# Modulation's products on GpSimd, their sums a step later on ScalarE

## The chip, the cores and the metric

One core of a Trainium2 chip runs the kernel. The metric is device time in microseconds. The core's engines each work through an instruction queue of their own: TensorE (PE; its weight loads are listed as PEld), VectorE (DVE), ScalarE (ACT), GpSimd (POOL) and SyncE (SP), which issues nearly all DMAs.

## What is computed

Two blocks follow each other on a sequence of 256 positions of width 1024. The first has two layers: a retention layer (4 heads, chunks of 128) and a causal latent-attention layer (16 heads, low-rank queries and keys); after each comes a normalised residual and a gated per-layer embedding, `x + (p @ w_proj) * sigmoid(x @ w_gate)`. The second block is modulated: six vectors of 1024 come from a conditioning vector c, and scale, shift and gate what follows.

```python
mod = jax.nn.silu(c) @ w_ada[l] + b_ada[l]
sh1, sc1, g1, sh2, sc2, g2 = jnp.split(mod, N_MOD, axis=-1)
h = layer_norm(x) * (1.0 + sc1[:, None]) + sh1[:, None]
proj = h @ w_in[l]
...
x = layer_norm(ALPHA * x + g1[:, None] * mix, ln1_g[l], ln1_b[l])
h = layer_norm(x) * (1.0 + sc2[:, None]) + sh2[:, None]
```

The change concerns the first line alone. `silu(c) @ w_ada` is a product of one row with a matrix of 1024 x 6144. Its first result is needed when the second block starts; the values of the second half of the block are needed late.

## The kernel before

Activations lie transposed: 128 features on the partitions, 256 positions along the free axis, in blocks of two or four such tiles. Every large matrix product in fp32 is made of three matmuls in a rounded format: each operand is split into a rounded part `hi` and the rest `lo`, and `mm` (L235ff) multiplies hi by hi, hi by lo and lo by hi. For each 128x1024 tile of weights SP loads `raw` (L165), ACT rounds it to `wh` (L178), and DVE subtracts to `wl` (L179); each has five or six buffers. Activations are split in the same way (L187 on ACT, L188 on DVE).

Modulation is not done on PE. `ada_steps` is a generator of 48 steps. Each holds one 128x1024 tile of the modulation weights (`adach`, two buffers, loaded over SP in program order), in which each partition has one output's 1024 weights. One DVE instruction multiplies it by silu(c), which lies in `siluc` on all partitions, and sums along the row into one column of `mod` (L413); after each eighth column the bias is added (L418). A call of `ada()` takes the next step; the very first call only issues two loads.

When a step comes is set by a clock that the program keeps while it is written down: `tick` adds each matmul's estimated time, and calls `ada()` when `mods["rate"]` microseconds of it have passed since the last step, up to a limit of 41 calls. `mod_rate` sets the rate at each stage: 10 at the start, 1.8 in the out-projection of the retention layer, 7.61 and then 12.84 in latent attention, 2.27 in its out-projection. A loop ahead of the second block takes what is left up to the limit, and `late_steps` takes eight further calls during the last stage. The final order on each engine is made by a scheduler from this program order and the dependencies; loads marked `keep_in_program_order` keep theirs on SP.

In the profiled execution 26 of the 48 L413 run in the first 204 us (start and retention layer), 16 in the latent-attention layer up to 397 us, none between there and 759 us, and six from there to 813 us.

The names in the rows: `ps` is a PSUM bank, `half` an activation block or half of a split, `t` a temporary, `sm` a softmax tile, `mod` the modulation's columns, `xs` (in the code) the input of the second block scaled by modulation, `php` the split per-layer embedding.

Of the kernel before, what the change touches and what calls it, by code (L numbers as in the profile page):

```python
# [14 lines left out]
AF = mybir.ActivationFunctionType  # L15
ALU = mybir.AluOpType
ADD, SUB, MUL = ALU.add, ALU.subtract, ALU.mult
# [65 lines left out]
def tile_kernel(ctx, tc, order, xT, pT, pos, vec, cst, cv, rows, wada, wts, outT):  # L83
    nc = tc.nc
    V, A, T = nc.vector, nc.scalar, nc.tensor
# [11 lines left out]
    def nm(s):  # L97
        uid[0] += 1
        return f"{s}_{uid[0]}"
# [26 lines left out]
    def two(nb):  # L126
        return Blk(nb, F32R), Blk(nb, F32R)
# [29 lines left out]
    def fetch(entries, width, parts=True, step=D, pinned=False):  # L157
        g = len(order)
        order.append((width, list(entries)))
        n = len(entries) * width  # L160
        tag, bufs = (("raw", 6), ("wh", 5), ("wl", 5))[0 if parts else [0, 1][g % len([0, 1])]]
        raw = wp.tile([P, D], F32, tag=tag, name=nm("raw"), bufs=bufs)
        for o in range(0, n, step):
            e = min(n, o + step)
            d = nc.sync.dma_start(out=raw[:, o:e], in_=wts[g, :, o:e])  # L165
            if pinned:
                tc.keep_in_program_order(d)
        return raw[:, :n]
# [13 lines left out]
    def nouter(name, ms, kbs, c0=0):  # L182
        return [(name, kb * P, c0 + m * P) for m in ms for kb in kbs]
# [15 lines left out]
    clk = [0.0]  # L199
# [3 lines left out]
    def after(us, fn):  # L203
        queue.append((clk[0] + us, fn))
        queue.sort(key=lambda e: e[0])


    mods = {"rate": None, "last": 0.0, "n": 0}

    def mod_rate(us):  # L210
        mods["rate"], mods["last"] = us, clk[0]

    def tick(us):
        clk[0] += us
        if busy[0]:
            return
        busy[0] = True
        if mods["rate"] and clk[0] - mods["last"] >= mods["rate"] and mods["n"] < 41:
            mods["last"] = clk[0]
            ada()  # L220
        while queue and queue[0][0] <= clk[0]:
            queue.pop(0)[1]()
        busy[0] = False

    def drain():
        busy[0] = True
        while queue:
            due, fn = queue.pop(0)
            clk[0] = max(clk[0], due)
            fn()  # L230
        busy[0] = False
# [4 lines left out]
    def mm(ps, l, r, first, last):  # L236
        T.matmul(ps, l[0], r[0], start=first, stop=False)  # L237
        T.matmul(ps, l[0], r[1], start=False, stop=False)  # L238
        T.matmul(ps, l[1], r[0], start=False, stop=last)  # L239
        tick(3 * cols(r[0]) / 2400.0)  # L240
# [5 lines left out]
    def rhs(pair, kb):  # L246
        return pair[0][kb], pair[1][kb]
# [35 lines left out]
    def col(name, i, n=1):  # L283
        o = VOFF[name] + i
        return vc[:, o:o + n]
# [111 lines left out]
        return t.unsqueeze(1).to_broadcast([P, n, S])  # L397


    mod = cp.tile([P, 48], F32, name="mod")  # L400
    sc = cp.tile([P, D], F32, name="siluc")

    def ada_steps():
        def fetch(n):
            ch = sp.tile([P, D], F32, tag="ada1", name=nm("adach"), bufs=2)
            tc.keep_in_program_order(nc.sync.dma_start(out=ch, in_=wada[n * P:(n + 1) * P, :]))
            return ch

        have = [fetch(0), fetch(1)]
        yield  # L410
        for n in range(48):
            ch = have.pop(0)
            V.tensor_tensor_reduce(ch, ch, sc, 1.0, 0.0, MUL, ADD, mod[:, n:n + 1])  # L413
            if n + 2 < 48:
                have.append(fetch(n + 2))
            if n % 8 == 7:
                m = slice(n - 7, n + 1)
                V.tensor_add(mod[:, m], mod[:, m], col("b_ada_2", n - 7, 8))  # L418
            yield

    ada_it = ada_steps()
# [9 lines left out]
    def ada():  # L431
        mods["n"] += 1
        next(ada_it, None)
# [80 lines left out]

    after(12.0, silu_c)
    after(18.0, ada)
    after(30.0, lambda: mod_rate(10))
    after(40.0, trig4)

    ret_g = two(16)  # L520
# [100 lines left out]
    def out_proj(name, pairs, ka, rate, done, layer):  # L621
        ys = proj_banks()
        mod_rate(rate)
        seq = Seq(nouter(name, range(8), range(ka)) + nouter(name, range(8), range(ka, 16)))
        for m in range(8):
            for kb in range(ka):
                mm(ys.at(m), seq.next(), rhs(pairs, kb), ys.starts(m) and kb == 0, False)
        drain()
        mod_rate(None)
        prep = ple_proj(layer)  # L630
        for m in range(8):
            for kb in range(ka, 16):
                mm(ys.at(m), seq.next(), rhs(pairs, kb), False, kb == 15 and ys.ends(m))
            if ys.ends(m):
                done(m, ys)
        return ys, prep
# [83 lines left out]
    def ple_proj(layer):  # L720
        php = [tp.tile([P, 2, S], F32R, tag="fa", name=nm("php"), bufs=3) for _ in range(2)]
        raw = t2()
        nc.gpsimd.dma_start(out=raw, in_=pT[:, 2 * layer:2 * layer + 2, :])
        split(php[0], php[1], raw)

        def prepared():
            seq = Seq(nouter(f"ple_proj{layer}", range(8), range(2)))
            tiles = [seq.next() for _ in range(16)]
            prj = Blk(DB)
            for i in range(4):  # L730
                ps = bank2()
                for b in range(2):
                    for kb in range(2):
                        mm(ps[:, b, :], tiles[(2 * i + b) * 2 + kb], (php[0][:, kb, :], php[1][:, kb, :]), kb == 0, kb == 1)
                A.copy(prj.pair(i), ps)
            return prj
        return prepared

    sums, done = proj_sums(False, lambda m, ys: ys.piece(m), "r")
    ys, prep = out_proj("ret_out", ret_g, 12, 1.8, done, 0)  # L740
    xt = post(xt, ys, sums, 0, prep)


# [78 lines left out]
    def mla_gate(p):  # L822

        if p % 2 == 0:
            sgs[p // 2] = Blk(4)
        ps = bank2()
        for b in range(2):
            for kb in range(8):
                mm(ps[:, b, :], seq_g.next(), rhs(xp, kb), kb == 0, kb == 7)
        gr = t2()  # L830
        V.scalar_tensor_tensor(gr, ps, -0.5, bc2(r1["nr"]), MUL, MUL)
        A.activation(sgs[p // 2].pair(p % 2), gr, AF.Silu)

    mla_g = two(16)
# [104 lines left out]
        V.tensor_mul(gt, pso, sgs[p // 2].pair(p % 2))  # L939
        split(mla_g[0].pair(p), mla_g[1].pair(p), gt)  # L940

    mod_rate(7.61)
    ng = 0
    for p in range(8):
        while ng < [2, 4, 6, 8, 8, 8, 8, 8][p]:
            mla_gate(ng)
            ng += 1
        if p == 4:
            mod_rate(12.84)
        mla_proj(p)  # L950
        after(3.07, lambda p=p: mla_scores(p))

    sums, done = proj_sums(False, lambda m, ys: ys.piece(m), "m")
    ys, prep = out_proj("mla_out", mla_g, 12, 2.27, done, 1)
    xt = post(xt, ys, sums, 1, prep)

    while mods["n"] < 41:
        ada()  # L960
    s1 = cp.tile([P, 16], F32, name="s1")
    ms = cp.tile([P, 16], F32, name="ms")
# [544 lines left out]
```

## Time and profile before

| what | value |
|---|---|
| median of 3 runs | 853.06 us (850.65 to 853.61) |
| the profiled execution, its own time | 847.85 us |
| its span, first to last instruction | 846.1 us |
| mean granted clock of TensorE in it | 0.997 of full speed |
| busy: PE, DVE, ACT, POOL | 826.1, 703.1, 555.2, 9.9 us |
| DMA | 167.48 MB, mean 198 GB/s |

The profile is of one execution. Its tables give an engine's busy time, the idle time ahead of a group of instructions, and what ended that idle time (`<-DVE t L331`: the result t of DVE's instruction of line 331). An engine's idle time matters where PE in turn waits for it.

### The profile page before, as it was taken

The numbers are of one execution on the slowest core, as the hardware profiler recorded it, in microseconds if no ns is written. First come the engines' busy times: TensorE is split into PE (matmuls) and PEld (weight loads), VectorE is DVE, ScalarE is ACT, GpSimd is POOL, SyncE is SP. The second block draws the span as 40 slices with busy tenths as digits, with TensorE's granted clock in tenths as the row PEclk, the third lists the DMA queues.
The fourth block names the chain that finished last, engine by engine and source line by source line (L and its number), as shares of the span: only waits on it lengthen the run. The fifth ranks groups of instructions, "written<-read, shape, count | busy, mean of one in ns | idle before, by whom it ended". The sixth has DMA issues, their size and how long they took to land.

```text
span 846.1 us, 15771 instructions
## 1 busy us (share of the span) xinstructions
PE 826.1 (98%) x6114; PEld 787.9 (93%) x6114; DVE 703.1 (83%) x1283; ACT 555.2 (66%) x968; POOL 9.9 (1%) x30
## 2 busy tenths in 40 slices
PE   8999999999999999998999999999999999999995
PEld 6989999999999989998999999999998999999885
DVE  6999798988889978688874768899677888889986
ACT  7655565545676686777754857999756576666550
POOL 0000000000000000000000000000000000000001
PEclk9999999999999999999999999999999999999998
DMA  9875567778556637374255364245463455567722
GB/s 335 323 258 212 215 217 269 255 264 319 171 182 248 223 145 259 116 263 145 99 184 176 121 224 152 98 150 199 148 224 128 134 190 191 184 214 255 277 77 75
DMA packets 46634, 167.48 MB, mean 198 GB/s; under 512 B 5216, under 2 KB 5472, under 8 KB 46560
## 3 DMA queue, kind: packets, MB, share of 16 engines
q1 hardware_dynamic: 45936, 164.38, 55.1%
q0 software_dynamic: 624, 2.10, 0.9%
q8 instruction: 48, 0.79, 0.4%
q14 instruction: 26, 0.21, 0.1%
HBM read 165.41 MB, written 1.05 MB: 197 GB/s over the span
## 4 chain that ended last, share of the span: by engine, by line
PE 50%; DVE 2%; ACT 1%; issue 1%; DVEq 0%
PE ps L238 13%; PE ps L237 13%; PE ps L239 13%; PE ps L243 10%; PE ps L341 1%; PE ps L363 0%; DVE wl L179 0%; PE ps L920 0%; PE ps L1170 0%; DVE t L1434 0%; DVE sm L1415 0%; DVE half L690 0%; DVE t L1411 0%; DVE t L1412 0%; PE ps L1407 0%
## 5 line engine op out<-in xcount | busy, mean ns | idle before, releaser
L237 PE MATMUL ps<-half,wh 128*128 128x256 f32 x1504 | 425.4, 284 | 1.4 <-ACT half L187 1.4
L238 PE MATMUL ps<-half,wh 128*128 128x256 f32 x1504 | 423.8, 282 | 0.6 <-DVE half L188 0.5
L239 PE MATMUL ps<-half,wl 128*128 128x256 f32 x1504 | 422.0, 281 | 1.1 <-DVE wl L179 1.0
L178 ACT CAST wh<-raw 128x1024 fp32r<-128x1024 f32 x233 | 243.5, 1049 | 154.9 <-PE ps L238 94.8
L179 DVE TENSOR_TENSOR wl<-raw,wh 128x1024 fp32r<-128x1024 f32 x233 | 282.7, 1219 | 59.5 <-ACT wh L178 57.3
L239 PEld LDWEIGHTS ps<-half,wl 128*128 128x128 f32 x1504 | 283.8, 189 | 1.7 <-DVE wl L179 1.7
L238 PEld LDWEIGHTS ps<-half,wh 128*128 128x128 f32 x1504 | 283.4, 188 | 1.9 <-DVE half L188 1.0
L237 PEld LDWEIGHTS ps<-half,wh 128*128 128x128 f32 x1504 | 282.5, 188 | 2.6 <-ACT half L187 2.0
L243 PE MATMUL ps<-half,raw 128*128 128x256 f32 (+2 forms) x384 | 84.9, 380 | 0.0
L243 PEld LDWEIGHTS ps<-half,raw 128*128 128x128 f32 x384 | 72.5, 190 | 10.0
L237 PE MATMUL ps<-wh,half 128*128 128x512 f32 (+1 forms) x202 | 72.6, 360 | 0.9 <-ACT wh L178 0.9
L413 DVE CUSTOM_DVE_ANT_0 adach<-adach,siluc 128x1024 f32<-128x1024 f32 x48 | 58.4, 1218 | 16.7 <-DMA adach<-in_wada 16.7
L238 PE MATMUL ps<-wl,half 128*128 128x512 f32 (+1 forms) x202 | 71.0, 351 | 0.5 <-DVE wl L179 0.5
L239 PE MATMUL ps<-wh,half 128*128 128x512 f32 (+1 forms) x202 | 71.0, 352 | 0.0
L1087 ACT ACTIVATE t<-apad,vec 128x256 f32<-128x256 f32 x106 | 44.3, 501 | 0.5 <-DVE half L1088 0.5
L237 PEld LDWEIGHTS ps<-wh,half 128*128 128x128 f32 x202 | 37.9, 188 | 6.8 <-ACT wh L178 1.7
L238 PEld LDWEIGHTS ps<-wl,half 128*128 128x128 f32 x202 | 38.1, 189 | 6.0 <-DVE wl L179 1.0
L239 PEld LDWEIGHTS ps<-wh,half 128*128 128x128 f32 x202 | 38.0, 188 | 5.6
L1088 DVE TENSOR_TENSOR half<-half,t 128x512 f32<-128x512 f32 x53 | 36.5, 689 | 3.7 <-ACT t L1087 1.8
L187 ACT CAST half<-t 128x256 fp32r<-128x256 f32 (+1 forms) x47 | 20.3, 453 | 17.9 <-DVE t L1347 10.9
L188 DVE TENSOR_TENSOR half<-t,half 128x256 fp32r<-128x256 f32 (+1 forms) x47 | 21.7, 482 | 4.5 <-ACT half L187 3.6
L1342 ACT ACTIVATE t<-ps,vec 128x256 f32<-128x256 f32 x38 | 21.0, 558 | 2.0 <-PE ps L239 1.2
(290 smaller groups left out, 908.1 us busy)
## 6 DMA issues: line engine op xcount, KB each, us to landing
raw<-in_wts SPq DMA_DIRECT2D x257, 512.0 KB, 4.1
adach<-in_wada SPq DMA_DIRECT2D x48, 512.0 KB, 5.0
half<-in_xT SPq DMA_DIRECT2D x4, 256.0 KB, 5.7
half<-in_rows POOLq DMA_DIRECT2D x2, 512.0 KB, 4.7
out<-t SPq DMA_DIRECT2D x4, 256.0 KB, 2.0
cst<-in_cst SPq DMA_DIRECT2D x1, 928.0 KB, 10.6
raw<-in_wts SPq DMA_DIRECT2D x2, 256.0 KB, 4.4
siluc<-in_cv SPq DMA_DIRECT2D x1, 512.0 KB, 9.0
```

The costliest lines, as they stand in the source:

```text
L178: A.copy(hi, raw)
L179: V.tensor_sub(lo, raw, hi.bitcast(F32))
L187: A.copy(hi, src)
L188: V.tensor_sub(lo, src, hi.bitcast(F32))
L237: T.matmul(ps, l[0], r[0], start=first, stop=False)
L238: T.matmul(ps, l[0], r[1], start=False, stop=False)
L239: T.matmul(ps, l[1], r[0], start=False, stop=last)
L243: T.matmul(ps, w, r, start=first, stop=last)
L413: V.tensor_tensor_reduce(ch, ch, sc, 1.0, 0.0, MUL, ADD, mod[:, n:n + 1])
L1087: A.activation(t[:, b, :], apad[:, i0 + b, k:k + S], AF.Copy, scale=w[b])
L1088: V.tensor_add(acc.pair(i0 // 2), acc.pair(i0 // 2), t)
L1342: A.activation(t[:, b, :], ps[:, b, :], AF.Identity, bias=col("b_dw_f_2", m), scale=w[2])
```

## The change

The step is cut in two. GpSimd takes the product, in place: `nc.gpsimd.tensor_mul(ch[n], ch[n], sc)`. At the next step ACT copies the product tile onto itself with an accumulator that sums the row into `mod` (`add_up`), and only then is the load of tile n + 2 issued, into the buffer that has come free. There are therefore 49 steps behind the first call. The limits go from 41 to 42, and the rates change: 10 to 9 at the start, 1.8 to 4.5, 7.61 (and 12.84 from the fifth pair of heads) to 10.5 throughout, 2.27 to 4.5.

```diff
-        if mods["rate"] and clk[0] - mods["last"] >= mods["rate"] and mods["n"] < 41:
+        if mods["rate"] and clk[0] - mods["last"] >= mods["rate"] and mods["n"] < 42:
...
-        have = [fetch(0), fetch(1)]
-        yield
-        for n in range(48):
-            ch = have.pop(0)
-            V.tensor_tensor_reduce(ch, ch, sc, 1.0, 0.0, MUL, ADD, mod[:, n:n + 1])
+        def add_up(n):
+            A.activation(ch[n], ch[n], AF.Copy, accum_out=mod[:, n:n + 1])
             if n + 2 < 48:
-                have.append(fetch(n + 2))
+                ch[n + 2] = fetch(n + 2)
             if n % 8 == 7:
                 m = slice(n - 7, n + 1)
                 V.tensor_add(mod[:, m], mod[:, m], col("b_ada_2", n - 7, 8))
+
+        ch = {n: fetch(n) for n in range(2)}
+        yield
+        for n in range(49):
+            if n > 0:
+                add_up(n - 1)
+            if n < 48:
+                nc.gpsimd.tensor_mul(ch[n], ch[n], sc)
             yield
...
-    after(30.0, lambda: mod_rate(10))
+    after(30.0, lambda: mod_rate(9))
...
-    ys, prep = out_proj("ret_out", ret_g, 12, 1.8, done, 0)
+    ys, prep = out_proj("ret_out", ret_g, 12, 4.5, done, 0)
...
-    mod_rate(7.61)
+    mod_rate(10.5)
...
-        if p == 4:
-            mod_rate(12.84)
...
-    ys, prep = out_proj("mla_out", mla_g, 12, 2.27, done, 1)
+    ys, prep = out_proj("mla_out", mla_g, 12, 4.5, done, 1)
...
-    while mods["n"] < 41:
+    while mods["n"] < 42:
         ada()
```

Lines behind the edit move down by four to six: L789 and L792 become L795 and L798, L697 becomes L703, L735 becomes L741, L1036 becomes L1040. The sum is L411 and the product L424.

Of the 48 steps, 18 now stand in the start and the retention layer, 18 in the latent-attention layer and its out-projection, six in the second gated embedding, and six in the last stage.

The first place is DVE's queue in the low-rank query chain of the latent-attention layer. Before (`adach` is the modulation tile; L367 to L373 are the Newton step of the normalisation, L789 and L792 scale the queries):

```order
L367 TENSOR_TENSOR t_507_3054<-t_505_3051 128x256
L179 TENSOR_TENSOR wl_3258<-raw_3255,wh_3257 128x1024
L372 SCALAR_TENSOR_TENSOR t_508_3056<-t_504_3049,t_507_3054 128x256
L413 ISA adach_3469,mod<-adach_3469,siluc 128x1024
L413 ISA mod 128x1
L373 SCALAR_TENSOR_TENSOR t_506_3053<-t_508_3056,t_505_3051 128x256
L300 TENSOR_TENSOR t_526_3206<-t_526_3206,t_527_3208 128x512
L789 TENSOR_TENSOR t_509_3059<-t_506_3053,t_490_2973 128x256
L179 TENSOR_TENSOR wl_3330<-raw_3327,wh_3329 128x1024
L792 SCALAR_TENSOR_TENSOR t_510_3061<-ps_2844,gq,t_509_3059 128x256
```

The same place of the changed kernel:

```order
L372 SCALAR_TENSOR_TENSOR t_498_3042<-t_494_3035,t_497_3040 128x256
L373 SCALAR_TENSOR_TENSOR t_496_3039<-t_498_3042,t_495_3037 128x256
L179 TENSOR_TENSOR wl_3214<-raw_3211,wh_3213 128x1024
L188 TENSOR_TENSOR kr_2824<-t_484_2972,kr_2823 64x256 x2
L795 TENSOR_TENSOR t_499_3045<-t_496_3039,t_480_2959 128x256
L179 TENSOR_TENSOR wl_3244<-raw_3241,wh_3243 128x1024
L798 SCALAR_TENSOR_TENSOR t_500_3047<-ps_2830,gq,t_499_3045 128x256
```

The L413 between L372 and L373 is gone; no modulation instruction stands in this queue any more but the bias.

The second place is ACT's queue at the start of the second gate projection, where the gate's input is split (L187, `half<-half`). Before:

```order
L735 COPY half_5999<-ps_6015 128x512
L735 COPY half_6000<-ps_6029 128x512
L187 CAST half_6057<-half_5967 128x256 x2
L178 CAST wh_6220<-raw_6218 128x1024
L735 COPY half_6000<-ps_6043 128x512
L187 CAST half_6057<-half_5967 128x512
L178 CAST wh_6250<-raw_6248 128x1024
L187 CAST half_6058<-half_5968 128x512
```

The same place of the changed kernel:

```order
L741 COPY half_6015<-ps_6031 128x512
L411 ACTIVATE adach_6369,mod<-adach_6369 128x1024
L741 COPY half_6016<-ps_6045 128x512
L187 CAST half_6073<-half_5983 128x256
L741 COPY half_6016<-ps_6059 128x512
L187 CAST half_6073<-half_5983 128x256
L178 CAST wh_6236<-raw_6234 128x1024
L187 CAST half_6073<-half_5983 128x512
L187 CAST half_6074<-half_5984 128x512
L411 ACTIVATE adach_6373,mod<-adach_6373 128x1024
L178 CAST wh_6266<-raw_6264 128x1024
```

Two sums have come into this stretch, the first of them ahead of the first piece of the split. Four more follow further down in the gate, the last two next to each other ahead of a weight cast.

The third place is SP's queue of loads, at the end of the weights of the same gate. Before (`raw` are weights):

```order
L165 DMA raw_6283<-in_wts 128x1024
L165 DMA raw_6318<-in_wts 128x1024
L165 DMA raw_6387<-in_wts 128x1024
L165 DMA raw_6444<-in_wts 128x1024
L165 DMA raw_6541<-in_wts 128x1024
```

The same place of the changed kernel:

```order
L165 DMA raw_6299<-in_wts 128x1024
L165 DMA raw_6334<-in_wts 128x1024
L407 DMA adach_6369<-in_wada 128x1024
L407 DMA adach_6373<-in_wada 128x1024
L165 DMA raw_6428<-in_wts 128x1024
L407 DMA adach_6377<-in_wada 128x1024
L407 DMA adach_6381<-in_wada 128x1024
L165 DMA raw_6485<-in_wts 128x1024
L407 DMA adach_6385<-in_wada 128x1024
L165 DMA raw_6582<-in_wts 128x1024
L407 DMA adach_6389<-in_wada 128x1024
```

Six modulation tiles now stand between the weights of the second block, each waiting for the sum that frees its buffer.

## Rows read from the trace of the kernel before

**Rows 1.** Page: busy time, share of the span and instructions of each engine.

```profile
PE 826.1 (98%) x6114; PEld 787.9 (93%) x6114; DVE 703.1 (83%) x1283; ACT 555.2 (66%) x968; POOL 9.9 (1%) x30
```

**Rows 2.** Waits of PE: line, releaser: us in total, times, longest.

```profile
PE ps L920 <- DVE sm L909: 2.8, 3, 1.7
PE ps L237 <- ACT half L187: 1.4, 1, 1.4
PE ps L341 <- DVE t L331: 1.1, 1, 1.1
```

**Rows 3.** Groups: line, engine, operation, out<-in, count | busy, mean ns | idle before.

```profile
L178 ACT CAST wh<-raw 128x1024 fp32r<-128x1024 f32 x233 | 243.5, 1049 | 154.9 <-PE ps L238 94.8 <-issue 28.1 <-PE ps L239 23.3
...
L413 DVE CUSTOM_DVE_ANT_0 adach<-adach,siluc 128x1024 f32<-128x1024 f32 x48 | 58.4, 1218 | 16.7 <-DMA adach<-in_wada 16.7
...
L902 ACT ACTIVATION_READ_ACCUMULATOR sm<-sm,sm 128x1 f32 x16 | 3.0, 187 | 0.0
```

**Rows 4.** Timeline, DVE and PE, 199 to 210: start, us, [idle before <-releaser].

```profile
202.25 1.22 DVE L413 CUSTOM_DVE_ANT_0 adach<-adach,siluc 128x1024 f32<-128x1024 f32 x1
...
209.37 1.53 PE L341 MATMUL ps<-t,ones 128*128 128x256 f32 x6 [1.09 <-DVE t L331]
```

**Rows 5.** Timeline, DVE and PE, 275 to 281.

```profile
276.18 1.22 DVE L413 CUSTOM_DVE_ANT_0 adach<-adach,siluc 128x1024 f32<-128x1024 f32 x1
...
280.19 0.62 PE L237 MATMUL ps<-half,wh 128*128 128x256 f32 x3 [1.37 <-ACT half L187]
```

**Rows 6.** Timeline, DVE and PE, 328 to 333.

```profile
329.00 1.21 DVE L413 CUSTOM_DVE_ANT_0 adach<-adach,siluc 128x1024 f32<-128x1024 f32 x1
...
331.90 0.61 PE L920 MATMUL ps<-ident,sm 128*128 128x128 f32 x3 [0.55 <-DVE sm L909]
```

**Rows 7.** Timeline, DVE and PE, 382 to 387.

```profile
382.85 1.23 DVE L413 CUSTOM_DVE_ANT_0 adach<-adach,siluc 128x1024 f32<-128x1024 f32 x1 [0.55 <-DMA adach<-in_wada]
...
386.67 0.49 PE L243 MATMUL ps<-a,t 128*128 128x128 f32 x2 [0.93 <-ACT a L925]
```

**Rows 8.** Timeline, DVE and PE, 395 to 398.

```profile
395.75 1.20 DVE L413 CUSTOM_DVE_ANT_0 adach<-adach,siluc 128x1024 f32<-128x1024 f32 x1
...
397.30 0.30 PE L920 MATMUL ps<-ident,sm 128*128 128x128 f32 x1 [1.75 <-DVE sm L909]
```

**Rows 9.** Windows: length, busy of PE, PEld, DVE, ACT, POOL, clock, DMA share.

```profile
255.00:397.00 142.00, 136.15 (x1121) 133.61 (x1120) 117.53 (x252) 105.04 (x203) 0.20 (x1) 1.00 0.57 200
```

**Rows 10.** Timeline, POOL (836 to 838, then to 842) and DVE.

```profile
836.93 1.74 POOL L1432 TENSOR_TENSOR t<-t,half 128x512 f32<-128x512 f32 x1 [12.65 <-DVE t L1431]
836.93 2.96 POOL L1432 TENSOR_TENSOR t<-t,half 128x512 f32<-128x512 f32 x2 [12.65 <-DVE t L1431]
...
839.66 0.78 DVE L1434 SCALAR_TENSOR_TENSOR t<-t,sm,half 128x512 f32<-128x512 f32 x1
...
840.43 0.74 DVE L1434 SCALAR_TENSOR_TENSOR t<-t,sm,half 128x512 f32<-128x512 f32 x1
```

**Rows 11.** Timeline, SP, ACT and PE, 470 to 506, around the second gate.

```profile
472.48 31.67 SPq L165 DMA_DIRECT2D raw<-in_wts  x11
...
480.26 0.74 ACT L187 CAST half<-half 128x256 fp32r<-128x256 f32 x2 [0.23 <-DVE half L691]
...
481.50 0.39 PE L238 MATMUL ps<-half,wh 128*128 128x256 f32 x1 [0.28 <-DVE half L188]
...
503.09 1.70 ACT L1036 ACTIVATE half<-half,s 128x256 f32<-128x256 f32 x4
...
504.23 2.12 PE L243 MATMUL ps<-half,raw 128*128 128x258 f32 x9
```

**Rows 12.** Page: DMA issues of the modulation tiles, KB each, us to landing.

```profile
adach<-in_wada SPq DMA_DIRECT2D x48, 512.0 KB, 5.0
```

**Rows 13.** Timeline, ACT and PE, 17 to 34.

```profile
23.36 2.18 ACT L178 CAST wh<-raw 128x1024 fp32r<-128x1024 f32 x2
...
30.67 0.28 PE L237 MATMUL ps<-half,wh 128*128 128x256 f32 x1
```

## The prediction

> **What bounds the kernel now.** I read the page's busy shares first. TensorE (PE) is busy for 826.1 us, 98% of the span [rows 1]: every microsecond that the change gains must be one in which PE stands still, and every microsecond that it costs must make PE stand still. So the second view is PE's waits [rows 2]. Together they are small: the three largest make 2.8 + 1.4 + 1.1 = 5.3 us, all on VectorE (DVE) or ScalarE (ACT). The third view is the groups of instructions: the product with its sum, L413, is 48 instructions of 1218 ns on DVE, 58.4 us in all [rows 3]. DVE is busy for 703.1 us of 846.1 and ACT for 555.2 [rows 1], so 58 us leave an engine at 83% and go to engines at 1% and 66%. That says little by itself, since DVE is not the bound; the question is which of PE's waits stand behind an L413. I looked for these in the timelines, and found five.
>
> - At 209.37 PE has idled 1.09 us for the squares' sum t of L331; L413 ran at 202.25 in a DVE queue that stays full from there on [rows 4].
> - At 280.19 it has idled 1.37 us; the L413 of 276.18 took DVE for 1.22 us in the middle of the chain that makes the operand [rows 5].
> - At 331.90: 0.55 us, behind the L413 of 329.00 [rows 6].
> - At 386.67: 0.93 us, behind the L413 of 382.85 [rows 7].
> - At 397.30: 1.75 us, of which the L413 of 395.75 makes 1.20 [rows 8].
>
> Together 1.09 + 1.22 + 0.55 + 0.93 + 1.20 = 5.0 us, 0.6% of the span. That is **all that can be won** by taking L413 off DVE; the other 43 of them cost PE nothing that the trace shows.
>
> **The change part by part.** The sum is made against the profiled execution (847.85 us, of which 846.1 is the span); that execution lies 0.6% under the median of the runs, 853.06. I carry the difference over to the median as it is.
>
> *L413 leaves DVE.* 58.4 us of DVE go. The first gap: in the changed order the last 30 us of the retention layer's out-projection hold no modulation step at all, so its 1.09 us should go, -1.1. The other four lie between 255 and 397 us, in the latent-attention layer: 1.22 + 0.55 + 0.93 + 1.20 = 3.9 us at most.
>
> *The sum goes to ACT.* An activation over 128x1024 with an accumulator is not in the trace. Its parts are: a 1024-wide pass takes 1049 ns (L178), reading an accumulator 187 ns (L902) [rows 3], so 1.24 us; 48 of them are 60 us, and ACT goes from 66% to 73%. Of these, 18 fall to the latent-attention layer. There ACT is busy for 105.04 of 142 us already [rows 9], and it makes operands that PE waits for (the exponentials, the copies, the first halves of the splits). A sum that stands in its queue just ahead of such an instruction delays it by up to 1.24 us; one that stands elsewhere costs nothing. From no hit (0) to six (7.4 us) is possible. I take two of 18, since a quarter of ACT's time there is free: +2.5. The layer comes to -3.9 + 2.5 = -1.4.
>
> *The product goes to GpSimd (POOL).* The nearest row is its 128x512 product-like add at L1432: the first takes 1.74 us while DVE is at work, both together 2.96, so the second took 1.22 [rows 10]. A 128x1024 product is then 2.4 us, and 3.5 us beside a busy DVE; 48 are 117 to 167 us on an engine that does nothing else, which is no bound. A step now takes load (5.0 us, [rows 12]) + 2.4 + 1.24 = 8.7 us with two buffers, where it took 5.0 + 1.2. As long as steps come every 9 us or more this hides.
>
> *What it does to DVE* is seen in one place: an L1434 that starts during the second POOL add takes 0.78 us, the next one, which meets none, 0.74 [rows 10]. So DVE loses 0.04 us; over 48 products that is 2 us in no place that PE waits for. I take 0, and leave a full block to a rival.
>
> *The steps are spread anew, but not evenly.* The rates and the limit of 42 leave six steps to the loop that empties what is left ahead of the last stage. In the changed order their six loads stand behind the weights of the second gate projection, and all six sums fall into that gate, where no step was before. The last weight load ahead of them leaves at 472.48 [rows 11]; two loads follow, land at about 478, and the first product ends at 478 + 2.4 = 480.4 or later, its sum at 481.7. In ACT's queue this sum stands ahead of the first L187 that splits the gate's input, which ran at 480.26; one copy stands between. PE had 0.28 us of waiting for the second half of this split [rows 11], so it has no slack: the first gate matmul comes 1 to 2 us late, say 1.5. The other sums come in pairs, 8.7 us apart: the last pair would be done at 473 + 3 x 8.7 = 499 to 502. They stand in ACT's queue ahead of a weight cast and of the L1036 activations that ran at 503.09 and feed PE at 504.23 [rows 11]. That is just in time or late by up to 3; I take 1.5. The burst: **+3.0**, between 0.5 and 9.
>
> *The start.* Two sums now stand ahead of the weight casts that ran at 23.36 [rows 13]; the products can't be there before the loads are. PE reads these weights at 30.67 [rows 13], some 7 us after, and the two sums and two evictions move them by 6 to 7. +0.5, between 0 and 2.
>
> The sum: -1.1 - 1.4 + 0 + 3.0 + 0.5 = **+1.0 us**: 848.9 for an execution like the profiled one, 854.1 beside the median.
>
> **The rivals.** *The gaps go and nothing comes instead.* ACT's 26% of free time takes all 18 sums, and the burst's sums find their products ready. Then -5.0 and 848.1 us. For it: 43 of 48 L413 cost PE nothing, so most places have slack. Against it: the first sum of the burst stands ahead of an instruction with no slack.
>
> *DVE and POOL shut each other out: slower.* DVE's work in the latent-attention layer is 117.53 us of 142 [rows 9], some 16 L413 among it (19.5 us). If DVE stood still for the whole of each of 18 products (44 us), it would have 117.5 - 19.5 + 44 = 142 us of work: it would be full, and PE would wait on it. Point from which it decides: a product that costs DVE more than the 1.22 us of the old L413 turns the gain round. Then no gap of the layer goes (0 for -3.9), and the two hits stay (+2.5); the products in the gate's burst meet DVE in its chain of normalisation and splits, two of 2.4 us ahead of the split: 3.0 + 4.8; with -1.1 and +0.5 about +7 to +10, so 860 to 863 us, or about 858 with half the block. For it: the first POOL add took 0.52 us more than the second, while DVE ran. Against it: there POOL lost, and DVE's 0.78 for 0.74 is next to nothing.
> [...]
>
> *The burst costs its upper end.* With 3.5 us a product, and loads that take twice the median among the weights, a round is 10 + 3.5 + 1.24 = 15 us; from 473 the third ends at 517, not 502. Sums at ACT's head then hold up its casts and the L1036 for as long, though the weights' five buffers hide some; PE loses 6 to 9 us: 859 to 862. Point from which it decides: the last sum ending after about 502. Against it: it needs both a product and a load at their worst, three rounds in a row; the median load takes 5.0 us [rows 12].
>
> *The change doesn't spread.* It holds in part already: six steps stand in one gate. It has no further price.
>
> **How the numbers follow.** Forecast, within half a per cent: 0.48. Gaps gone, nothing instead: 0.18. Shut out: 0.22. Burst at its upper end: 0.12. A difference of under 0.5% (4.3 us) is about what a measurement of this kernel can't tell from none: 848.8 to 857.3. Faster by more, 0.17 (the first rival ends right at the bound; nearly all of its chance, and the tail of the forecast); slower by more, 0.34; the same, 0.49. The range goes from 847.8 (the first rival and a little run-to-run scatter) to 861.5 (the shut-out at two thirds, most of the burst).
>
> **What would show it.** Right: no L413 on DVE; PE's waits on L331, on the low-rank chain and on the softmax gone or shorter; sums L411 of about 1.24 us; products L424 of 2.4 to 3.5 us; a new PE wait of 1 to 2 us at the start of the second gate and one ahead of the L1040 activations. Wrong: L179 longer than 1.22 us beside the products (shut out); PE waiting on DMA or ACT for over 4 us in the gate (burst); PE idle for under 16 of the 20 us that it idles now (gaps gone).

## The result, and the profile after

The changed kernel takes **914.49 us** (median of 4 runs, 911.66 to 920.02) where the kernel before takes 853.12: a ratio of 1.0733, 95% interval 1.0671 to 1.0796. That is 61 us slower, where I had forecast +1.0 us, a range up to 861.5 and a chance of 0.34 for slower. The direction had been a rival's; the size lies far outside the range.

The profiled execution of the changed kernel (911.66 us) begins its page so, to be laid beside [rows 1]; the second line is the granted clock in 40 slices of the span:

```profile
PE 848.9 (93%) x6114; PEld 804.4 (88%) x6114; DVE 726.5 (80%) x1187; ACT 601.5 (66%) x1064; POOL 141.8 (16%) x78
...
PEclk9999979999999799998999979999999999999998
```

The span is 909.8 us, 63.7 more than before. Two things make it. PE stands still for 909.8 - 848.9 = 60.9 us, where it stood for 846.1 - 826.1 = 20.0: +40.9. And the same 6114 matmuls are busy for 22.8 us longer: the mean granted clock fell from 0.997 to 0.969, and the three slices with a 7 hold three of its four longest stops (8.07, 5.51, and 4.16 with 2.74 us, all shown below). DVE, from which 58.4 us of work were taken [rows 3], is busy for *longer* than before: 726.5 us, where it was 703.1 [rows 1].

PE's waits (line, releaser: us in total, times, longest), to be laid beside [rows 2]:

```profile
PE ps L237 <- ACT t L187: 14.2, 3, 8.1
PE ps L237 <- ACT half L187: 9.7, 2, 5.5
PE ps L926 <- DVE sm L915: 8.8, 6, 2.8
PE ps L238 <- DVE wl L179: 5.9, 7, 2.5
PE ps L239 <- DVE wl L179: 3.7, 3, 1.7
PE ps L238 <- DVE half L188: 3.0, 2, 2.7
```

Behind them stand the groups of instructions:

```profile
L179 DVE TENSOR_TENSOR wl<-raw,wh 128x1024 fp32r<-128x1024 f32 x233 | 312.1, 1346 | 77.5 <-ACT wh L178 75.6
...
L424 POOL TENSOR_TENSOR adach<-adach,siluc 128x1024 f32<-128x1024 f32 x48 | 132.0, 2752 | 653.0 <-DMA adach<-in_wada 411.5
L411 ACT ACTIVATE adach<-adach 128x1024 f32<-128x1024 f32 x48 | 50.8, 1059 | 81.2 <-POOL adach L424 81.1
```

Before, the first of these groups read:

```profile
L179 DVE TENSOR_TENSOR wl<-raw,wh 128x1024 fp32r<-128x1024 f32 x233 | 282.7, 1219 | 59.5 <-ACT wh L178 57.3
```

The same 233 weight splits L179 took 282.7 us on DVE before and take 312.1 now, though nothing in them changed. And ACT stands still for 81 us in front of the sums, for products that are not done. These two observations gave two theories. **A**: GpSimd's products shut DVE out of SBUF, where `adach` and the weight tiles lie. **B**: ACT stands at the head of its queue at a sum, with everything behind it, until a late load and its product are done.

What A looks like is seen at the start of the second gate, on POOL, DVE and PE (start, us, instruction, idle before):

```profile
522.97 4.90 POOL L424 TENSOR_TENSOR adach<-adach,siluc 128x1024 f32<-128x1024 f32 x2 [42.10 <-DMA adach<-in_wada]
...
523.02 2.64 DVE L367 TENSOR_TENSOR t<-t 128x256 f32<-128x256 f32 x1 [0.54 <-ACT t L381]
525.70 2.46 DVE L370 TENSOR_TENSOR t<-t,t 128x256 f32<-128x256 f32 x1
528.19 0.43 DVE L373 SCALAR_TENSOR_TENSOR t<-t,t 128x256 f32<-128x256 f32 x1
...
530.30 0.80 PE L237 MATMUL ps<-half,wh 128*128 128x256 f32 x2 [4.16 <-ACT half L187]
...
533.84 0.58 PE L238 MATMUL ps<-half,wh 128*128 128x256 f32 x1 [2.74 <-DVE half L188]
```

L367 and L370 are instructions of 0.42 us. Each starts just after a product has started, and ends about when that product ends: 2.64 and 2.46 us. L373, which comes when POOL is free, takes its 0.43. The chain makes PE's next operand, and PE stands for 4.16 and then 2.74 us.

In the cases below it matters who comes first, and where the operands lie. At 414.68 us an L915 on an SBUF tile starts 0.3 us after a product and is held until it ends; the L902 just ahead of it, which reads from PSUM (`<-ps`) and runs inside the same product, takes 0.27 us. At 126 us the product comes while DVE is in a split of weights, and it is the product that takes 3.66 us, while an L554 that reads PSUM beside it takes its usual 0.69. At 309.76 the product, undisturbed 2.39 us, takes 5.46: two L188 and two L179 that start *after* it keep their usual length, so by POOL's record it let them all pass, up to 312.97:

```profile
414.38 2.39 POOL L424 TENSOR_TENSOR adach<-adach,siluc 128x1024 f32<-128x1024 f32 x1 [10.08 <-ACT sm L908]
...
414.49 0.27 DVE L902 CUSTOM_DVE_ANT_0 sm<-ps,cst 128x128 f32<-128x128 f32 x1
...
414.68 2.43 DVE L915 TENSOR_SCALAR sm<-sm,sm 128x128 f32<-128x128 f32 x2
...
126.00 3.66 POOL L424 TENSOR_TENSOR adach<-adach,siluc 128x1024 f32<-128x1024 f32 x1 [10.50 <-DMA adach<-in_wada]
...
125.56 1.23 DVE L179 TENSOR_TENSOR wl<-raw,wh 128x1024 fp32r<-128x1024 f32 x1
...
127.56 0.69 DVE L554 SCALAR_TENSOR_TENSOR t<-ps,t 128x512 f32<-128x512 f32 x1
...
309.76 5.46 POOL L424 TENSOR_TENSOR adach<-adach,siluc 128x1024 f32<-128x1024 f32 x1 [8.72 <-DMA adach<-in_wada]
...
309.27 1.43 DVE L188 TENSOR_TENSOR half<-t,half 128x256 fp32r<-128x256 f32 x4
310.61 2.36 DVE L179 TENSOR_TENSOR wl<-raw,wh 128x1024 fp32r<-128x1024 f32 x2
```

What B looks like is the longest of PE's waits, in the retention layer; SP, ACT and PE:

```profile
121.32 0.42 SPq L407 DMA_DIRECT2D adach<-in_wada  x1
...
122.14 1.05 ACT L178 CAST wh<-raw 128x1024 fp32r<-128x1024 f32 x1
129.69 1.06 ACT L411 ACTIVATE adach<-adach 128x1024 f32<-128x1024 f32 x1 [6.49 <-POOL adach L424]
...
130.74 0.39 ACT L187 CAST t<-t 128x256 fp32r<-128x256 f32 x1
...
131.18 0.58 PE L237 MATMUL ps<-t,t 128*128 128x256 f32 x1 [8.07 <-ACT t L187]
```

The load of the tile leaves at 121.32, behind weight loads on SP; the product can begin at 126.00, is held up by DVE and ends at 129.66; ACT has stood at the sum since 123.2, and the small L187 behind it is what PE waits for. DVE had its input ready at 127.46 (L568, late itself), so the last 3.3 us of PE's 8.07 are ACT's standing and the sum itself. Before that PE waited for DVE, which had been late since the product before: that one held an L188 from 113.15 for 2.90 us, and ACT at its sum until 115.54. The windows show the clock then: 0.50 of full speed for the next 4 us, after 8.07 us of standing still. (Columns: busy us of PE, PEld, DVE, ACT, POOL, granted clock, DMA share, GB/s.)

```profile
120.00:131.00 11.00, 3.12 (x25) 2.79 (x24) 8.15 (x12) 4.08 (x7) 3.66 (x1) 0.75 0.67 238
131.00:135.00 4.00, 3.82 (x17) 3.82 (x18) 2.21 (x3) 3.13 (x5) 0.00 (x0) 0.50 0.14 41
```

The second longest wait, in the latent-attention layer, shows B at a product that meets nobody. It takes 2.39 us as soon as its load is in; ACT stands at its sum for 8.21 us, the normalisation's L792 behind it makes DVE stand for 6.49, and PE for 5.51:

```profile
298.65 2.39 POOL L424 TENSOR_TENSOR adach<-adach,siluc 128x1024 f32<-128x1024 f32 x1 [16.15 <-DMA adach<-in_wada]
...
301.08 1.06 ACT L411 ACTIVATE adach<-adach 128x1024 f32<-128x1024 f32 x1 [8.21 <-POOL adach L424]
...
302.66 0.43 DVE L367 TENSOR_TENSOR t<-t 128x256 f32<-128x256 f32 x1 [6.49 <-ACT t L792]
...
306.62 0.58 PE L237 MATMUL ps<-half,wh 128*128 128x256 f32 x1 [5.51 <-ACT half L187]
```

### The profile page after: what moved, and what is told of

It is laid out like the page before. It is cut to its first block, busy times and chain, and to the rows that moved or that the text cites. A ratio compares the mean times of both kernels' runs of the same rounds, so it can differ in the third digit from the quotient of the medians.

```text
span 909.8 us, 15864 instructions
## 1 busy us (share of the span) xinstructions
PE 848.9 (93%) x6114; PEld 804.4 (88%) x6114; DVE 726.5 (80%) x1187; ACT 601.5 (66%) x1064; POOL 141.8 (16%) x78
## 4 chain that ended last, share of the span: by engine, by line
PE 52%; DVE 12%; DMA 6%; ACT 5%; issue 3%; POOL 3%; SPq 0%; DVEq 0%; POOLq 0%; ACTq 0%
PE ps L238 14%; PE ps L237 13%; PE ps L239 13%; PE ps L243 9%; DMA adach<-in_wada 4%; DVE wl L179 4%; POOL adach L424 3%; ACT wh L178 1%; PE ps L341 1%; DMA g<-mod 1%; DVE half L188 1%; DVE t L1315 1%; ACT adach L411 1%; DVE half L696 1%; PE ps L363 1%
## 5 line engine op out<-in xcount | busy, mean ns | idle before, releaser
L237 PE MATMUL ps<-half,wh 128*128 128x256 f32 x1504 | 431.3, 288 | 9.7 <-ACT half L187 9.7
L238 PE MATMUL ps<-half,wh 128*128 128x256 f32 x1504 | 429.3, 286 | 3.2 <-DVE half L188 3.0
L239 PE MATMUL ps<-half,wl 128*128 128x256 f32 x1504 | 426.9, 284 | 3.7 <-DVE wl L179 3.7
L179 DVE TENSOR_TENSOR wl<-raw,wh 128x1024 fp32r<-128x1024 f32 x233 | 312.1, 1346 | 77.5 <-ACT wh L178 75.6
L237 PEld LDWEIGHTS ps<-half,wh 128*128 128x128 f32 x1504 | 288.5, 192 | 11.0 <-ACT half L187 10.5
L238 PEld LDWEIGHTS ps<-half,wh 128*128 128x128 f32 x1504 | 289.1, 192 | 4.9 <-DVE half L188 3.9
L239 PEld LDWEIGHTS ps<-half,wl 128*128 128x128 f32 x1504 | 289.2, 192 | 4.4 <-DVE wl L179 4.3
L424 POOL TENSOR_TENSOR adach<-adach,siluc 128x1024 f32<-128x1024 f32 x48 | 132.0, 2752 | 653.0 <-DMA adach<-in_wada 411.5
L411 ACT ACTIVATE adach<-adach 128x1024 f32<-128x1024 f32 x48 | 50.8, 1059 | 81.2 <-POOL adach L424 81.1
L187 ACT CAST half<-t 128x256 fp32r<-128x256 f32 (+1 forms) x47 | 20.4, 452 | 20.8 <-DVE t L1351 14.1
L188 DVE TENSOR_TENSOR half<-t,half 128x256 fp32r<-128x256 f32 (+1 forms) x47 | 27.7, 612 | 6.1 <-ACT half L187 5.3
```

Source lines behind the costliest of these rows:

```text
L179: V.tensor_sub(lo, raw, hi.bitcast(F32))
L187: A.copy(hi, src)
L188: V.tensor_sub(lo, src, hi.bitcast(F32))
L411: A.activation(ch[n], ch[n], AF.Copy, accum_out=mod[:, n:n + 1])
L424: nc.gpsimd.tensor_mul(ch[n], ch[n], sc)
```

## The experiments

Each run stood beside runs of the kernel before on its own chip. The differences below are against the median of those: 851.6 us for the products alone (e4), without sums (e2), without products (e7) and the product on DVE (e1); 851.8 for the rates (e5), the step (e6), the four pieces (e8) and the first version of "What can be won" (e9); 851.0 for the pieces without sums (e11), only writing (e10) and the second version (e12); 852.7 for the eight columns (e13). Numbers in parentheses are 95% intervals of the ratio. In the cuts of code, `...` stands for lines left out.

### The products alone, in the kernel before

```diff
+    dump = cp.tile([P, 512], mybir.dt.bfloat16, name="dump")
...
             V.tensor_tensor_reduce(ch, ch, sc, 1.0, 0.0, MUL, ADD, mod[:, n:n + 1])
+            for o in (0, 512):
+                nc.gpsimd.tensor_mul(dump, sc[:, o:o + 512], mod[:, n:n + 1].to_broadcast([P, 512]))
```

> The kernel before, its order on PE, ACT and SP unchanged; after each L413 GpSimd multiplies two 128x512 halves of siluc by the column just summed, into a tile that nobody reads. Nothing is left out. Theory A (GpSimd's products shut DVE out of SBUF): two-input DVE instructions that start during a product grow by up to 1.2 us; DVE busy rises by 40 to 70 us, and the time goes to 870 to 890 us, the rest of the loss after being the wait of B. Theory B (ACT stands at the head of its queue at a sum whose product waits for a late load, and the products themselves cost little): 853 to 856 us.

Measured: 898.73 us, +47 (ratio 1.0554, 1.0455 to 1.0653). DVE's busy time rose from 703.1 to 758.3 us, by 55; PE waits for DVE nearly everywhere (9.7 us for L179, 8.0 for the softmax, 7.5 for the sum of squares). Only three additions of the bias wait for these products, 5.0 us in all on DVE; the orders on PE, ACT and SP are those of before. The groups:

```profile
L179 DVE TENSOR_TENSOR wl<-raw,wh 128x1024 fp32r<-128x1024 f32 x233 | 306.1, 1320 | 51.8 <-ACT wh L178 49.9
...
L416 POOL TENSOR_TENSOR dump<-siluc,mod 128x512 bf16<-128x512 f32 x96 | 137.2, 1429 | 550.1 <-DVE mod L414 545.7
```

A holds, and more than I gave it: GpSimd's work whose result nobody uses costs 47 us.

### Products without sums

```diff
+    V.memset(mod, 0.0)
...
-            A.activation(ch[n], ch[n], AF.Copy, accum_out=mod[:, n:n + 1])
```

> The changed kernel without the sums on ACT: the products are taken on GpSimd and nobody sums them, the modulation columns stay at zero plus bias, so that part of the computation is left out. Theory A (shut out): the products are all there, so 880 to 910 us. Theory B (ACT waits at the sums): with no sum ACT never waits for a product, so 850 to 858 us. If both hold: in between, near 875.

Measured: 896.2 us, +44.6 (1.0439 to 1.061). The products alone cost three quarters of the loss, in the order of the changed kernel too; the 18 us to its 914.5 need the sums.

### Sums without products

```diff
-            if n < 48:
-                nc.gpsimd.tensor_mul(ch[n], ch[n], sc)
```

> The changed kernel without the products on GpSimd: ACT sums the weights as they were loaded, so the product with silu(c) is left out. Theory A (shut out): no product, no loss, 850 to 856 us, although ACT has 60 us of sums. Theory B: the sums still stand in ACT's queue and wait for late loads, by some 3 us less each than with a product between; ACT's wait at L411 stays at 30 to 60 us, and the time at 875 to 895 us.

Measured: 851.03 us, no difference (0.9973 to 1.0019). The sums are all there, 60 us of them on ACT. Its wait in front of the sums, and the weight split:

```profile
ACT adach L411 <- DMA adach<-in_wada: 30.6, 19, 3.6
...
L179 DVE TENSOR_TENSOR wl<-raw,wh 128x1024 fp32r<-128x1024 f32 x233 | 283.4, 1221 | 96.5 <-ACT wh L178 94.4
```

ACT stands at the head of its queue for 31 us, and the kernel is no slower than before. B alone, as I had put it (875 to 895 us), falls. So does the hope of a gain: DVE is busy for only 654.7 us here, and the kernel is no faster than before either. With what L413 is worth (the last run below), the sums on ACT and the new rates together cost PE about what L413 had cost it on DVE. At the sum that ACT stood at until 301.08 above, for 8.21 us, it stands for 3.10 here.

This run also tells where DVE's extra time in the changed kernel lies, 726.5 - 654.7 = 72 us. Of the instructions that both runs have, 39 are more than 0.15 us longer in the changed kernel than their kind is here in the mean. Each of the 39 overlaps a product in time, and together they are 74 us longer.

### The product on DVE, the sum on ACT

```diff
-                nc.gpsimd.tensor_mul(ch[n], ch[n], sc)
+                V.tensor_mul(ch[n], ch[n], sc)
```

> The changed kernel with the product on DVE instead of GpSimd, the sum on ACT a step later as in it. Theory A (shut out): GpSimd is idle, so nothing is blocked; 850 to 857 us. Theory B: the sum on ACT still waits for a product that waits for a late load, and DVE now waits for the load too; 875 to 900 us.

Measured: 858.8 us, +7 (1.0046 to 1.0088). Just above A's 850 to 857 and far from B's. Now both engines carry a part, and PE waits for both; some 4 of the 7 us are the new rates' (next run).

### The rates alone, and the step alone

The step of before with the rates of after:

> The step of before (product and sum in one DVE instruction) with the rates and the limit of after. Nothing is left out. If GpSimd's products are the whole loss: the gap that the retention layer's end had is gone and the burst of six costs DVE 7 us in the gate, 849 to 855 us. If the new places of the steps (the burst in the second gate) cost by themselves: 856 to 862.

Measured: 855.75 us, ratio 1.0041 (1.0020 to 1.0063). The rates by themselves cost some 4 us, at the seam of the two ranges that I had put. In its trace PE stands for 3.95 us at 484.71, at the start of the second gate, behind two of the steps on DVE (L414 in this kernel) that fell into the normalisation's chain: the burst costs without GpSimd too.

The step of after with the rates of before (and the limit of 42):

> The step of after with the rates of before (the limit stays at 42, as the sum of each step comes one call later). Nothing is left out. The products are as many, so if they are the loss it stays: 895 to 925 us. Steps come every 1.8 us in the retention layer's out-projection, too fast for a load, a product and a sum with two buffers: if ACT's waits at the sums matter, more than after, 915 to 930; if they don't, 895 to 905.

Measured: 909.89 us (1.0659 to 1.0717). It lies between my two ranges (895 to 905, 915 to 930). Where the products are put matters little; that they are there matters.

### Products in four pieces

```diff
-                nc.gpsimd.tensor_mul(ch[n], ch[n], sc)
+                for o in range(0, D, 256):
+                    nc.gpsimd.tensor_mul(ch[n][:, o:o + 256], ch[n][:, o:o + 256], sc[:, o:o + 256])
```

> The changed kernel with each product cut into four of 128x256. Nothing is left out. If an instruction keeps the other engine out for its whole length, DVE now waits 0.6 us at most at a time instead of 2.3 and passes between two pieces: L179 back near 1.25 us, POOL's spans longer, 870 to 895 us. [...]

Measured: 928.19 us, +76 (1.0874 to 1.0932): slower still, which neither theory had said. Its groups and ACT's wait:

```profile
L179 DVE TENSOR_TENSOR wl<-raw,wh 128x1024 fp32r<-128x1024 f32 x233 | 290.6, 1254 | 90.9 <-ACT wh L178 88.8
...
L425 POOL TENSOR_TENSOR adach<-adach,siluc 128x256 f32<-128x256 f32 x192 | 175.2, 943 | 631.5 <-DMA adach<-in_wada 400.7 <-ACT t L1347 194.9 <-ACT t L885 14.4
...
ACT adach L411 <- POOL adach L425: 107.5, 35, 8.1
```

The part on DVE went as A says: L179 is back near its 1.22 us, and DVE's extra time over the run without products fell from 726.5 - 654.7 = 72 us to 695.5 - 654.7 = 41. But now GpSimd takes longer: the four pieces of a product take 175.2 / 48 = 3.65 us instead of 2.75 (whether they wait for DVE or cost a start each isn't shown), and ACT's wait for it rose from 81.1 to 107.5 us. So I formed a third theory, **A with B**: the block costs DVE time, DVE's and GpSimd's lateness makes the products late, and ACT, which stands at the sum, hands that lateness on to the weight casts and splits behind it.

### The same pieces, without sums

> Products in four pieces of 128x256 as in e8_four_pieces, and no sums on ACT as in e2_no_sum; the sums are left out. In e8 the DVE's extra time fell from 74 to 40 us and yet the time rose, while ACT's wait at the sums rose from 81 to 107 us. If that wait is what ate the gain, this run without sums shows the gain: 870 to 882 us against 896 of e2. If shorter pieces bring nothing, 893 to 900.

Measured: 875.23 us (1.0232 to 1.0317), as this theory said: 21 us better than whole products without sums, and 53 better than with sums. Shorter pieces do help DVE (busy for 707.9 us, 731.6 with whole products and no sums); it was the sums that took it back.

### GpSimd as long, but only writing

```diff
-                nc.gpsimd.tensor_mul(ch[n], ch[n], sc)
+                nc.gpsimd.memset(ch[n], 0.5)
+                nc.gpsimd.memset(ch[n], 0.25)
+                nc.gpsimd.memset(ch[n][:, :512], 0.125)
```

> The changed kernel with each product replaced by three memsets of the same tile on GpSimd (1024, 1024 and 512 columns, some 2.4 us together), so GpSimd takes as long, the sums wait for it as before, but it reads nothing from SBUF. The product is left out. If it is GpSimd's reading that shuts DVE out, L179 stays at 1.22 us. Then the run shows the wait at the sums by itself: 851 to 856 us if the lateness of a product alone costs nothing, 860 to 880 if ACT's standing at the sums costs by itself. If writing shuts DVE out as well: 900 to 920.

Measured: 853.89 us, +2.9 (1.0007 to 1.0055). GpSimd works for 46.1 + 45.9 + 25.4 = 117 us, as long as 48 undisturbed products of 2.4 us, and each sum waits for it. DVE's weight splits take what they take without products (1221 ns):

```profile
L425 POOL MEMSET adach<- 128x1024 f32 x48 | 46.1, 961 | 2.5
...
L179 DVE TENSOR_TENSOR wl<-raw,wh 128x1024 fp32r<-128x1024 f32 x233 | 283.4, 1221 | 89.5 <-ACT wh L178 87.2
...
ACT adach L411 <- POOL adach L426: 32.4, 20, 3.7
```

So 117 us of GpSimd's *writing* leave the splits at 1221 ns, where the products, which also read two SBUF tiles, brought them to 1346; I take the reading for the cause, though the products also multiply, and no run tells the two apart. And the chain of load, 2.4 us on another engine, and sum is nearly harmless as long as the splits keep their length: ACT waits 32 us for it, not 81. But memsets are not free for all of DVE. It is busy for 660.4 us, 5.7 more than without products (e7). Of this 2.0 us lie in the softmax's L917, a TENSOR_SCALAR on one SBUF tile: 377 ns in the mean, 315 without products; PE waits for it five times, 7.0 us in all. At 413.08 two L917 (0.28 and 0.35 us in the run without products) take 0.95 us and end just behind a memset that ends at 413.82; PE waits 1.38 us for them:

```profile
412.87 0.95 POOL L424 MEMSET adach<- 128x1024 f32 x1 [2.08 <-ACT sm L910]
...
413.08 0.95 DVE L917 TENSOR_SCALAR sm<-sm,sm 128x128 f32<-128x128 f32 x2
...
414.05 0.52 PE L928 MATMUL ps<-ident,sm 128*128 128x128 f32 x3 [1.38 <-DVE sm L917]
```

### What can be won at all

Two versions take the steps out of the latent-attention layer and keep them on DVE. The first (its edit is below) puts them into its out-projection, and the rest falls into the second gate; the second moves this rest on into the second block's projection.

```diff
-    mod_rate(7.61)
...
-        if p == 4:
-            mod_rate(12.84)
...
-    ys, prep = out_proj("mla_out", mla_g, 12, 2.27, done, 1)
+    ys, prep = out_proj("mla_out", mla_g, 12, 3.4, done, 1)
```

> The kernel before with no modulation step in the latent-attention layer; its steps go to that layer's out-projection (one each 3.4 us) and the rest into the second gate. Nothing is left out. If the four gaps behind L413 in that layer are worth what they were read as (3.9 us), 847 to 850 us; if what stands behind them is next in line at once, or the steps in the gate cost as much, 851 to 855.

> As e9_none_in_mla (step of before on DVE, none in the latent-attention layer), and the five steps that fell into the second gate are taken one at a time later, in the projection of the second block, ahead of the pointwise convolution. Nothing is left out. In e9 PE stood still for 4.1 us at that gate behind two L413 in the normalisation's chain, with a lower clock after it. If that goes and the projection has room on DVE: 842 to 846 us. If what the gate waits for is next in line, or DVE is too full there: 847 to 850.

Measured: 847.74 us (ratio 0.9959, 0.9940 to 0.9979) and 848.28 (0.9968, 0.9950 to 0.9987): both faster than the kernel before by 0.3 to 0.4%. In the second the 4.0 us at the gate are gone from the list of waits, but 2.0 us for an L1083 have come in the second block, and no gain over the first can be measured: what the gate gave, the projection took.

Last, L413 over eight of its 1024 columns, in the kernel before:

```diff
-            V.tensor_tensor_reduce(ch, ch, sc, 1.0, 0.0, MUL, ADD, mod[:, n:n + 1])
+            V.tensor_tensor_reduce(ch[:, :8], ch[:, :8], sc[:, :8], 1.0, 0.0, MUL, ADD, mod[:, n:n + 1])
```

> The kernel before with its rates, L413 over the first eight of the 1024 columns only: loads, waits and number of steps stay, but nearly all of DVE's 58 us of modulation is left out, and nothing is put on another engine. If the five gaps are all that L413 costs PE (5.0 us): 845 to 849 us. If L413 costs more than the waits behind it show: under 844. If what stands behind the gaps is next in line at once: 850 to 853.

Measured: 841.76 us (0.9832 to 0.9916), 11 us under the median of before beside it; its profiled execution, 842.35, is 5.5 us under the profiled one of before, 847.85, which is not among the runs beside it. The expectation "under 844" holds: L413 costs more than the waits behind it show. All of modulation's arithmetic is worth some 5 to 11 us.

## Why the prediction was wrong

*What bounds the kernel, and what can be won.* PE's idle time was the right measure. The five gaps made 5.0 us. In e13's profiled execution PE stands still for 840.3 - 826.4 = 13.9 us instead of 20.0, so the reading was right for the execution that was read. By the medians it is 11 us, so it was low as a bound for the kernel.

*L413 leaves DVE.* In the retention layer the wait on L331 went, as said. In the latent-attention layer the softmax's waits rose from 2.8 us in three to 8.8 in six. The sums alone don't do that: without products (e7) it is one wait of 1.3 us. With memsets (e10) they are 7.0 us in five, though no split is held; whether that comes from sums that wait for a late tile or from the small instructions that memsets hold isn't shown.

*The sum on ACT.* 1059 + 186 ns, where 1.24 us had been put together from two rows. The two hits of 18 (2.5 us) were too few, as far as can be said: e7 has all the sums and loses what it wins, and what it wins is worth 5 to 11 us (e13); of what it loses, some 4 us are the new rates'.

*The product on GpSimd.* 2.39 us undisturbed and 2.75 in the mean, within the 2.4 to 3.5. The size of the instruction was right. That this "is no bound" says too little: of the 42 DVE instructions with two SBUF inputs that start during a product in the changed kernel, 32 take longer than their kind and end only behind it, as L367 does at 523.02 (2.64 us for 0.42).

*What it does to DVE: the step that failed.* I took 0 from one pair of rows, an L1434 of 0.78 us beside one of 0.74 [rows 10]. The rows could not show more. GpSimd's second add ended at 836.93 + 2.96 = 839.89, and L1434 had begun at 839.66: they met for 0.23 us. I multiplied 0.04 us by 48 where I should have asked how long the overlap was, and the other row in the same group, with one beside it that I did not show, had answered:

```profile
836.17 1.38 DVE L1431 TENSOR_TENSOR t<-t,half 128x512 f32<-128x512 f32 x2
```

DVE's two L1431 went on until 837.55, 0.62 us into the first add, and that add took 0.52 us longer than the second, about as long as DVE went on. In the changed kernel 32 of 42 DVE instructions with two SBUF inputs that start during a product, and all eight TENSOR_SCALAR instructions on an SBUF tile that do, take longer than their kind takes in the kernel before, and end 0.02 to 1.09 us behind the product, for about 2 us more in the cases above. What I put at 0 measures 72 us of DVE's time, and products without sums make the kernel 44.6 us slower (e2), idle ones 47 (e4).
Where the operands lie shows in the same trace: L370, with its inputs in SBUF, took 2.46 us for 0.42, L554, with one input in PSUM, 0.69 beside a product; and beside memsets (e10) L179 kept its 1221 ns. Who came first decided in most of these cases, not in all: at 309.76 four DVE instructions that started after the product seem to have gone ahead of it.

*The rival "shut each other out".* Its mechanism and the place at the gate were right, two products ahead of the split. Its price, +7 to +10, was not. Its sum counts 16 L413 in the latent-attention layer, as the section on the kernel before does (26, 16 and 6); in the trace they are 28, 14 and 6, which takes 2.4 us from the 19.5 and changes little. I let it work in the latent-attention layer and the gate only; but two-input instructions on DVE are everywhere, and the longest wait was in the retention layer, at 131.18. I left out that late products reach ACT's queue (896 without the sums, 914 with them), and that PE, after standing for 8.07 us, came back at a clock of 0.50 for 4 us (the longer matmuls make 22.8 us of the 63.7).

*A step of 8.7 us hides.* Wrong, for a queue that I did not count: the load stands behind weight loads on SP, which wait for buffers that DVE's splits free (SP waited 416.6 us for L179, in 152 waits). At 115.54 the sum before it ran; the load left at 121.32, when PE had begun 763 matmuls. Without products (e7), in the same order, the load of this tile left when PE had begun 720.

*The burst.* The place is right by luck, the cause wrong, the size low: 4.16 + 2.74 us of PE's waiting for the 1.5 I had taken. I had put it down to a sum ahead of L187 on ACT; that sum was done at 526.56, and the L187 at 529.84 waited 2.81 us for DVE's L697, whose chain the products held. Without GpSimd (e5) DVE is late there too, and PE waits 3.95. Nothing was lost at its end, the L1040 activations, where I had put the other 1.5.

*The start.* I took 0.5 us, up to 2. PE waited 1.66 us at 27.10 for an L179 that the second product held, and 1.27 at 34.36 for an L179 of usual length, when no product ran: 2.9 in all, on DVE and not on ACT as I had argued.

Open: how the 61 us divide between block and sums. Against the kernel before, in which L413 still costs its own 11 us, the sums make no difference without products, 18 us with whole ones and 53 with pieces. Counted from e13, where the arithmetic is nearly gone (and the rates are the old ones), products alone cost some 55 us, sums alone some 10, and both 72; so with whole products most of it adds up, and with pieces (35, 10 and 87) it does not. That the loop runs over SP (blocked DVE, late buffers, late loads, late products) is read from the trace at 121.32 and was not tried by itself.

## What to carry to other kernels

Work that goes to an idle engine isn't always free: here GpSimd's products, which read SBUF as DVE's splits do, cost 44.6 us with nobody waiting for them (e2), and writes of about the same length 2.9 (e10). Before GpSimd is given a job, count the busy engine's instructions with their operands in SBUF, and price each meeting at up to the whole length of the other's instruction (2.64 us for an instruction of 0.42 here). A row that is to show contention must first be asked how long the two overlapped; 0.23 us can't speak for 2.4. And an in-order queue turns another engine's lateness into its own, as ACT's did at its sum for 8.21 us: put the consumer of an uncertain product where nothing critical stands behind it.

## What the runs showed of the hardware

- Of the 42 DVE instructions with two SBUF inputs that started during one of GpSimd's 128x1024 products, 32 were held: they ended 0.02 to 1.09 us behind the product, and instructions of 0.42 us took 2.46 and 2.64. The other ten kept their usual length: four at 309.76, two at 126.00 (L567 and L568, 0.43 us), an L179 at 852.14 (1.22) and three that started in the product's last 0.1 us. All eight TENSOR_SCALAR instructions on one SBUF tile that started during a product were held too (L915, 2.43 us for two; an L905 of 0.16 us took 2.29 at 459.15). None of the 20 with an input in PSUM was (L902 0.27 us, L554 0.69), nor was an L910, a RECIPROCAL on one SBUF tile (0.17 us at 414.40).
- A product of 2.39 us undisturbed took 3.10 at 112.41, where it started in the middle of a weight split on DVE, and 5.46 at 309.76: the first seems to have waited for the split that it met, the second for four instructions more that started after it. What decides between the two isn't shown.
- Memsets on GpSimd of about the same total length (117 us) did nothing to DVE's two-input weight splits (L179: 1221 ns with them, 1219 before), but the TENSOR_SCALAR L917 took 377 ns in the mean beside them, 315 without; two at 413.08 took 0.95 us and ended just behind a memset.
- Four GpSimd pieces took 3.65 us together, one product 2.75; beside the pieces DVE's extra time was 41 us, beside whole products 72.
- After PE had stood for 8.07 us, its clock was granted at 0.50 of full speed for the next 4 us.
